# Decoder step: the last feed-forward's gate and up products of 18 slices as seven block products instead of eight

## The chip, the cores and the metric

The kernel runs on one core of a Trainium2 chip. The metric is the device time of one execution in microseconds (us). The engines have the names of the profile: PE (TensorE, matrix products), PEld (its weight loads), DVE (VectorE, elementwise), ACT (ScalarE, copies and functions), POOL (GpSimd), SP (the engine that issues nearly all transfers). PE reads its operands from the on-chip memory SBUF and writes to PSUM, eight banks of 2 KB per partition; DVE and ACT read both.

## The reference

A two-layer decoder step for one prompt of 1024 tokens and eight sample tokens, width 1024. Each layer is a mixer and then a feed-forward; the change touches only the second layer's feed-forward, for the second half of the prompt and the samples (512 + 8 = 520 columns).

```python
def swiglu(h, w_gu, w_down):
    gate, up = jnp.split(h @ w_gu, 2, axis=-1)
    return (jax.nn.silu(gate) * up) @ w_down
...
        h = h + rmsnorm(mix, g[1])
        h = h + rmsnorm(swiglu(rmsnorm(h, g[2]), w_gu[l], w_down[l]), g[3])
```

`w_gu` is 1024 x 5632 (2816 gate columns, then 2816 up columns), `w_down` 2816 x 1024. The 2816 columns are 22 slices of 128.

## The kernel before

**Layout and precision.** Activations are kept transposed: 128 features on the partitions, tokens along the row. Every fp32 operand of a product is split into a rounded high part (ACT) and the rest (DVE subtracts), and each 128x128 weight block takes three matmuls: high times high, high times low, low times high.

**Groups.** Group 0 is 512 prompt tokens, group 1 the other 512 and the 8 samples. A group-1 product is done as two column halves of 260, in the two banks of one PSUM tile.

**proj (L256 on)** makes one 128-row output: `split_w` (L240 on) loads the weights in tiles of four blocks (256 KB, SP queue, L245), splits them (L250 on ACT, L251 on DVE), and the matmuls of L264 follow. Five raw and five split weight tiles turn over (`wraw`, `wspl`).

**ffn.part (L464 on)** works through parts of 5, 5, 4, 4 and 4 slices. For a slice: gate product, SiLU (`silu`, L281 to L285: one DVE max, three ACT steps exp, ln, exp, one DVE product), up product, DVE product L474, split into the tile `m` (L271 on ACT, L272 on DVE). Then eight `w_down` products over the part's slices, added into the running sum `R` (L401 on ACT for the first part, L403 on DVE after it). `R` has one buffer for the whole kernel.

**PSUM.** Two tiles of two banks for products (`mmp`), three single banks (`smp`, `S()`) and one (`nsp`, `NS()`) for everything else.

**Order of work.** Pieces of the program are generators. `weave((a, na), (b, nb))` draws steps from both in the ratio na to nb, and `drain` runs one to its end. That is the program order, which a planner takes as priorities: with its own costs for every instruction it sets the order of each engine's queue, and the queues then run strictly in that order, with semaphores between them. Reuse of a buffer waits for the last reader of what was in it.

**The end of the program.** Around the change, in order: `f0.part(4)` of layer 1 for group 0, woven with `o1.finish` (which makes the input `x` of the last feed-forward); `f0.finish` (norm and residual, L384 and L390), `store_y` (transposes L1135 and the rows' store) and `token_rows` (transposes L440, L450), woven 22 to 18 with parts 0 and 1 of the last feed-forward `f1`; then `f1`'s parts 2, 3, 4, and `finish_rows`, which normalises and stores. Much earlier, layer 0's group-0 feed-forward is woven with the group-1 mixer.

POOL issues 32 indirect transfers for the sample cache (L731) and else nearly nothing.

Of the kernel before, what the change touches and what calls it, by code (L numbers as in the profile page):

```python
# [17 lines left out]
P = 128  # L18
# [4 lines left out]
def tile_decoder(  # L23
# [38 lines left out]
    mmp = pool("mmp", 2, space=PSUM)  # L62
    smp = pool("smp", 3, space=PSUM)
    nsp = pool("nsp", 1, space=PSUM)
# [15 lines left out]

    def NS():
        return nsp.tile([P, 512], F32, tag="ns", name=nm("ns"))
# [21 lines left out]
    def S():  # L104
        return smp.tile([P, 512], F32, tag="s", name=nm("s"))
# [209 lines left out]

    def wo_tiles(g):
        return [X(g) for _ in range(ND)]
# [136 lines left out]

    htok = []

    PARTS = [(0, 5), (5, 5), (10, 4), (14, 4), (18, 4)]

    class ffn:
# [4 lines left out]
        def part(self, pi):  # L464
# [18 lines left out]
            for m in range(ND):  # L483
                ps = proj(g, w_down[l], f0, nf, m * P, mids)
                evac_raw(g, self.R, ps, m, self.acc, pi == 0, last)
                if last and self.rows:
                    nc.scalar.activation(
                        self.R[m][:, :n], self.R[m][:, :n], AF.Copy, scale=gcol(l, 3, m)
                    )
                    if m == 3:  # L490
                        self.first_half()
# [11 lines left out]
        def first_half(self):  # L503
            self.yt = [xpool.tile([P, D], F32, tag="x0", name=nm("yT")) for _ in range(CH)]
            for c in range(CH):
                ps = S()
                for k in range(4):
                    nc.tensor.transpose(ps[:, k * P : (k + 1) * P], self.R[k][:, c * P : (c + 1) * P], ident)  # L508
                nc.scalar.copy(self.yt[c][:, :512], ps)
            self.ys = xpool.tile([P, D], F32, tag="x0", name=nm("yTs"))  # L510
            ps = S()
            for k in range(4):
                nc.tensor.transpose(ps[:NB, k * P : (k + 1) * P], self.R[k][:, G : G + NB], ident)
            nc.scalar.copy(self.ys[:NB, :512], ps[:NB, :])

        def finish_rows(self):

            ht, hsm = htok[0]
            g, R, acc = self.g, self.R, self.acc
            ps = NS()  # L520
            for c in range(CH):
                nc.tensor.matmul(ps[:, c : c + 1], acc[:, c * P : (c + 1) * P], ones[:, 0:1], start=True, stop=True)  # L522
            nc.tensor.matmul(ps[:NB, CH : CH + 1], acc[:, G : G + NB], ones[:, 0:1], start=True, stop=True)
            r = small([P, 8], tag="rr")
            nc.scalar.activation(r[:, :CH], ps[:, :CH], AF.Ln, scale=1.0 / D, bias=epsb)
            nc.scalar.activation(r[:, :CH], r[:, :CH], AF.Exp, scale=-0.5)
            rs = small([P, 8], tag="rr")
            nc.scalar.activation(rs[:NB, 0:1], ps[:NB, CH : CH + 1], AF.Ln, scale=1.0 / D, bias=epsb[:NB])
            nc.scalar.activation(rs[:NB, 0:1], rs[:NB, 0:1], AF.Exp, scale=-0.5)
            for c in range(CH + 1):  # L530
                prompt = c < CH
                n = P if prompt else NB
                yt, h = (self.yt[c], ht[c]) if prompt else (self.ys, hsm)
                rc = r[:, c : c + 1] if prompt else rs[:NB, 0:1]
                o = c * P
                pt = S()
                for k in range(4):
                    nc.tensor.transpose(pt[:n, k * P : (k + 1) * P], R[4 + k][:, o : o + n], ident)
                nc.vector.scalar_tensor_tensor(  # L539
                    yt[:n, :512], yt[:n, :512], rc, h[:n, :512], op0=ALU.mult, op1=ALU.add  # L540
                )
                nc.vector.scalar_tensor_tensor(  # L542
# [697 lines left out]
```

## Time and profile before

| | |
|---|---|
| median of 3 runs | 2549.02 us (2548.02 to 2551.21) |
| the profiled execution | 2551.36 us, span 2549.6 us, granted TensorE clock 0.996 |
| PE busy | 2518.9 us (99%), 15653 matmuls |
| DVE busy | 1557.2 us (61%) |
| ACT busy | 1186.6 us (47%) |
| POOL busy | 43.8 us (2%) |
| moved by DMA | 297.91 MB, mean 117 GB/s |

The span is the time from the first to the last instruction; the execution's own time is a little longer. Busy shares are means over stages of different kinds. In a group of instructions the first numbers are busy time and the mean of one in ns, and behind the bar stands the idle time of the engine just before them and what ended most of it. PE overlaps its matmuls, so the mean of one is longer than the step from one to the next; the step is the busy time of a stretch divided by its count. A row of the DMA queues has packets, MB and the share of 16 engines over the span that the packets took.

### The profile page before, as it was taken

To read this page: it belongs to the slowest core of one execution; us is meant where nothing else is said; L and a number is where in the kernel's file an instruction comes from. 1 tells how busy PE (TensorE), PEld (TensorE's weight loads), DVE (VectorE), ACT (ScalarE), POOL (GpSimd) and SP (SyncE) were. 2 spreads that over 40 slices of the span, in tenths; PEclk is the share of its full clock that TensorE was granted. 3 is DMA by queue.
4 is the path that set the end of the run, shared out by engine and by line. 5 is a ranking of instruction groups with operands and counts; after the bars stand their busy time and mean duration, and the time that the engine had idled before them with its cause. 6 is when DMAs were issued, how large, how long until landed. Compare 5 with 4: busy or idle time off the path is not lost. (4 is left out here: it accounts for less than half of the span.)

```text
span 2549.6 us, 40536 instructions
## 1 busy us (share of the span) xinstructions
PE 2518.9 (99%) x15653; PEld 2193.2 (86%) x15653; DVE 1557.2 (61%) x2714; ACT 1186.6 (47%) x2187; POOL 43.8 (2%) x59
## 2 busy tenths in 40 slices
PE   8999999999999999999999999999999999999998
PEld 6888898878877888999999989766776798999998
DVE  6666566654775677555544577667677558444445
ACT  6346543243443445555433455455555445443334
POOL 1000000000000000000000000011000000000000
PEclk9999999999999999999999999999999999999999
DMA  6352242233644445231333445453443244323332
GB/s 186 109 162 71 75 150 76 65 112 116 182 127 129 136 153 183 86 88 57 102 93 94 126 153 179 144 153 94 135 140 115 77 124 129 110 86 103 93 92 67
DMA packets 457708, 297.91 MB, mean 117 GB/s; under 512 B 17573, under 2 KB 422642, under 8 KB 457514
## 3 DMA queue, kind: packets, MB, share of 16 engines
q1 hardware_dynamic: 454954, 286.92, 37.6%
q0 software_dynamic: 2560, 8.39, 1.1%
q8 instruction: 123, 2.02, 0.3%
q14 instruction: 71, 0.58, 0.1%
HBM read 265.44 MB, written 29.80 MB: 116 GB/s over the span
## 5 line engine op out<-in xcount | busy, mean ns | idle before, releaser
L264 PE MATMUL mm<-x,ws 128*128 128x260 f32 (+1 forms) x10080 | 1668.4, 323 | 1.4 <-ACT x L355 1.3
L264 PEld LDWEIGHTS mm<-x,ws 128*128 128x128 f32 x10080 | 1443.1, 188 | 166.3 <-issue 29.2
L250 ACT CAST ws<-w 128x512 fp32r<-128x512 f32 (+1 forms) x800 | 475.5, 595 | 878.4 <-PE mm L264 801.3
L251 DVE TENSOR_TENSOR ws<-w,ws 128x512 fp32r<-128x512 f32 (+1 forms) x800 | 523.5, 657 | 324.0 <-ACT ws L250 314.6
L264 PE MATMUL mm<-m,ws 128*128 128x260 f32 (+1 forms) x3168 | 544.4, 326 | 0.1
L264 PEld LDWEIGHTS mm<-m,ws 128*128 128x128 f32 x3168 | 455.1, 189 | 53.9 <-issue 7.1
L403 DVE TENSOR_TENSOR r<-r,mm 128x520 f32<-128x520 f32 (+1 forms) x128 | 88.3, 690 | 99.2 <-PE mm L264 97.7
L281 DVE TENSOR_SCALAR t<-mm 128x512 f32<-128x512 f32 (+1 forms) x104 | 72.1, 693 | 102.5 <-PE mm L264 102.0
L474 DVE TENSOR_TENSOR t<-t,mm 128x512 f32<-128x512 f32 (+1 forms) x88 | 60.8, 691 | 117.2 <-PE mm L264 117.2
L285 DVE TENSOR_TENSOR t<-t,t 128x512 f32<-128x512 f32 (+1 forms) x88 | 61.1, 694 | 88.3 <-ACT t L284 88.1
L304 DVE TENSOR_TENSOR st<-st,n 128x512 f32<-128x512 f32 (+1 forms) x98 | 67.0, 690 | 6.9 <-ACT n L303 5.0
L272 DVE TENSOR_TENSOR m<-t,m 128x512 fp32r<-128x512 f32 (+1 forms) x88 | 61.0, 694 | 3.7 <-ACT m L271 1.6
L282 ACT ACTIVATE t<-t 128x512 f32<-128x512 f32 (+1 forms) x88 | 55.9, 635 | 14.9 <-DVE t L281 7.8
L271 ACT CAST m<-t 128x512 fp32r<-128x512 f32 (+1 forms) x88 | 54.8, 623 | 10.1 <-DVE t L474 2.8
L283 ACT ACTIVATE t<-t 128x512 f32<-128x512 f32 (+1 forms) x88 | 55.8, 635 | 2.6
L284 ACT ACTIVATE t<-t 128x512 f32<-128x512 f32 (+1 forms) x88 | 55.9, 635 | 2.4
L902 PEld LDWEIGHTS s<-a,a 128*128 128x128 f32 x448 | 53.4, 192 | 1.2
L902 PE MATMUL s<-a,a 128*128 128x64 f32 x448 | 53.2, 271 | 0.0
L1073 PE MATMUL s<-b,trir 128*128 128x512 f32 (+3 forms) x96 | 38.0, 397 | 7.6 <-DVE b L272 5.3
L731 POOL DMA_INDIRECT c<-in_cache_sb_k,pidx x16 | 16.2, 1015 | 1640.7 <-DVE x L272 790.4
L1037 DVE SCALAR_TENSOR_TENSOR b<-b,b 128x512 f32<-128x512 f32 (+3 forms) x48 | 26.7, 556 | 28.2 <-ACT b L1036 28.0
L1085 PE MATMUL s<-b,a 128*128 128x512 f32 (+3 forms) x96 | 41.6, 515 | 1.9 <-DVE b L1040 1.5
(298 smaller groups left out, 1940.2 us busy)
## 6 DMA issues: line engine op xcount, KB each, us to landing
w<-in_w_gu SPq DMA_DIRECT2D x352, 256.0 KB, 3.0
w<-in_w_down SPq DMA_DIRECT2D x160, 256.0 KB, 2.8
w<-in_w_in_a SPq DMA_DIRECT2D x80, 256.0 KB, 2.9
w<-in_w_o SPq DMA_DIRECT2D x64, 256.0 KB, 2.8
w<-in_w_mem_kv SPq DMA_DIRECT2D x32, 256.0 KB, 2.9
c<-in_cache_mem_k SPq DMA_DIRECT2D x16, 512.0 KB, 4.2
c<-in_cache_mem_v SPq DMA_DIRECT2D x16, 512.0 KB, 3.9
w<-in_w_kv SPq DMA_DIRECT2D x32, 256.0 KB, 3.1
```

The lines of the kernel that those rows point to most:

```text
L250: nc.scalar.copy(ws[:, 0, :n, :], raw[:, :n, :])
L251: nc.vector.tensor_sub(ws[:, 1, :n, :], raw[:, :n, :], ws[:, 0, :n, :].bitcast(F32))
L264: nc.tensor.matmul(ps[:, a, : PW[g]], wt, xt[k][:, xi, o : o + PW[g]], start=(k == 0 and wi == 0), stop=(k == nk - 1 and wi == 2),)
L272: nc.vector.tensor_sub(dst[1], src, dst[0].bitcast(F32))
L281: nc.vector.tensor_scalar(sv(x, g), pv(ps, g), -44.0, None, op0=ALU.max)
L282: nc.scalar.activation(d, x[:, :n], AF.Exp, scale=-1.0)
L284: nc.scalar.activation(d, d, AF.Exp, scale=-1.0)
L285: nc.vector.tensor_mul(d, d, x[:, :n])
L304: nc.vector.tensor_add(acc[:, :n], acc[:, :n], t[:, :n])
L403: nc.vector.tensor_add(dst, dst, pv(ps, g))
L474: nc.vector.tensor_mul(sv(sg, g), sv(sg, g), pv(pu, g))
L902: nc.tensor.matmul(plv[:, hh, c, :], K_[:, hh, cs], rhs, start=True, stop=True)
```

## The change

For 18 of the 22 slices, gate and up of a slice are no longer two products of 128 x 1024 by 1024 x 520. They are taken together as a two-by-two block product (gate and up rows; two halves of the 1024 inputs; two column halves of 260) and done with seven block products of 128 x 512 by 512 x 260 (Strassen's scheme in Winograd's form). A block product is 4 blocks x 3 matmuls = 12 matmuls, so a slice has 84 instead of 96.

- The four sums of weight blocks are made in DRAM: per part four tensors of 512 rows by the part's columns, by eight DMAs issued from POOL, four copies and four that add to what is there (`weight_sums`). They are woven into layer 0's group-0 feed-forward. Ahead of each part's eight, POOL copies one column of `f0.R[0]` (`mark`), behind which the eight are queued.
- The four sums of input blocks are made by DVE and split, for each of four row blocks (`sums_w`), behind slices 0, 1 and 2, whose products stay as they were in number (`gate_up_q`, slices 0 to 3).
- From slice 4 on, `gate_up_w` makes the slice: seven weight tiles of 256 KB (three from `w_gu`, four from the sums) instead of four, each split as before; partial results carried between PSUM banks by two negating ACT copies; two adds on DVE.
- All the PSUM pools are closed ahead of it and one of eight banks is opened (`quads`: four tags of two banks); `S()` and `NS()` take turns in two of the tags.
- SiLU is one ACT instruction for each half. From part 1 on, weight tiles also use buffers of the pools `a` and `c`.
- The weave of parts 0 and 1 with the work ahead goes from 22:18 to 17:7. `first_half` and `finish_rows` move out of the class unchanged; the down products use the banks of the new pool.

```diff
-    mmp = pool("mmp", 2, space=PSUM)
-    smp = pool("smp", 3, space=PSUM)
-    nsp = pool("nsp", 1, space=PSUM)
+    banks = ctx.enter_context(ExitStack())
+    mmp = banks.enter_context(tc.tile_pool(name="mmp", bufs=2, space=PSUM))
...
+    def Q(i):
+        return single[0].tile([P, 512], F32, tag=f"q{i}", name=nm("q"))
...
     def S():
+        if single:
+            turn[0] += 1
+            return Q(3 * (turn[0] % 2))
...
+    def sums_w(xs, ops):
+        n, h = NG[1], PW[1]
+        for k in range(4):
+            x0, x1 = xs[k], xs[k + 4]
...
+            def full(x, c):
+                t = B()
+                nc.vector.tensor_add(t[:, :h], x[:, 0, c : c + h].bitcast(F32), x[:, 1, c : c + h].bitcast(F32))
+                return t
+
+            b11, b12, b21, b22 = full(x0, 0), full(x0, h), full(x1, 0), full(x1, h)
+            for d, p, a, b in (
+                (b11, u[:, :, o : o + h], b12, b11), (b12, y[:, :, h : 2 * h], b12, b22),
+                (b22, y[:, :, :h], b22, b11), (b21, z[:, :, o : o + h], b21, b22),
+            ):
+                nc.vector.tensor_sub(d[:, :h], a[:, :h], b[:, :h])
+                split_to((p[:, 0, :], p[:, 1, :]), d[:, :h])
...
+    def gate_up_w(l, f, ops, spl, raws):
...
+        def product(ps, j, first=False):
+            w = split(weight(j))
+            i = src[j][1]
+            for k in range(4):
+                x = ops[k][i]
+                for wi, (wj, xi) in enumerate(((0, 0), (0, 1), (1, 0))):
+                    nc.tensor.matmul(
+                        ps[:, :h], w[:, wj, k * P : (k + 1) * P], x[:, xi, :],
+                        start=(first and k == 0 and wi == 0), stop=(k == 3 and wi == 2), skip_group_check=True,
+                    )
+
+        pa, pb, pc, pd = (Q(i) for i in range(4))
+        product(pa, 0, True)
+        nc.scalar.activation(pb[:, :h], pa[:, :h], AF.Copy, scale=-1.0)
+        product(pd, 1, True)
+        product(pb, 2)
+        nc.scalar.activation(pc[:, :h], pb[:, :h], AF.Copy, scale=-1.0)
+        product(pa, 3)
+        sg = T()
+        nc.scalar.activation(sg[:, :h], pa[:, :h], AF.Silu)
+        product(pb, 4)
+        dt = T()
+        nc.scalar.copy(dt[:, h:n], pd[:, :h])
+        gt = T()
+        nc.vector.tensor_add(gt[:, h:n], dt[:, h:n], pb[:, :h])
+        product(pc, 5)
+        nc.vector.tensor_sub(gt[:, :h], pc[:, :h], dt[:, h:n])
+        product(pb, 6)
+        nc.scalar.activation(sg[:, h:n], gt[:, :h], AF.Silu)
+        nc.vector.tensor_mul(sg[:, :h], sg[:, :h], pb[:, :h])
+        nc.vector.tensor_mul(sg[:, h:n], sg[:, h:n], gt[:, h:n])
...
+    def weight_sums(l, parts, after):
+        for i in parts:
+            mark = nc.gpsimd.tensor_copy(small([P, 1], tag="mk", bufs=1), after()[:, 0:1])
...
+            for d, a, add in (
+                (s3, a11, False), (s1, a21, False), (s3, a21, True), (s1, a22, True),
+                (s2, s3, False), (s2, a22, True), (s4, s2, False), (s4, a12, True),
+            ):
+                with tc.issue_after(mark.ins):
+                    if add:
+                        nc.gpsimd.dma_start(d, a, accum_op=ALU.add)
+                    else:
+                        nc.gpsimd.dma_start(d, a)
+                yield
...
+    class ffn_w:
...
+        def part(self, pi):
...
+                if f0 + j < self.plain:
+                    mt, ins = gate_up_q(l, f0 + j, self.x)
+                    mids.append(mt)
+                    with tc.issue_after(ins.ins):
+                        for _ in range((1, 2, 1, 0)[j]):
+                            next(self.sums, None)
+                else:
+                    mids.append(gate_up_w(l, f0 + j, self.ops, self.spl, self.raws))
...
-    weave((a1.sample(), 6), (a1.gate(), 4), (f0.part(1), 9))
-    weave((chain(a1.merge(), a1.mem()), 12), (a1.mem_sample(), 20), (chain(f0.part(2), f0.part(3)), 16))
-    drain(f0.part(4))
+    def running():
+        return f0.R[0]
+
+    weave((a1.sample(), 6), (a1.gate(), 4), (f0.part(1), 9), (weight_sums(1, (0,), running), 8))
+    weave(
+        (chain(a1.merge(), a1.mem()), 12), (a1.mem_sample(), 20), (chain(f0.part(2), f0.part(3)), 16),
+        (weight_sums(1, (1, 2), running), 16),
+    )
+    weave((f0.part(4), 8), (weight_sums(1, (3,4), running), 16))
...
-    f1 = ffn(1, 1, o1.x, True)
-    weave((chain(f0.finish(False), store_y(0, f0.R), token_rows(1, o1.R)), 22), (chain(f1.part(0), f1.part(1)), 18))
+    banks.close()
+    single.append(ctx.enter_context(tc.tile_pool(name="quads", bufs=2, space=PSUM)))
+    f1 = ffn_w(1, o1.x, 4)
+    weave((chain(f0.finish(False), store_y(0, f0.R), token_rows(1, o1.R)), 17), (chain(f1.part(0), f1.part(1)), 7))
     drain(f1.part(2), f1.part(3), f1.part(4), f1.finish_rows())
```

More of the change, by code (lines that the diff above doesn't have):

```diff
@@ L61, in tile_decoder @@
     cpool = pool("cpool", 4)
-    mmp = pool("mmp", 2, space=PSUM)
-    smp = pool("smp", 3, space=PSUM)
-    nsp = pool("nsp", 1, space=PSUM)
+    banks = ctx.enter_context(ExitStack())
+    mmp = banks.enter_context(tc.tile_pool(name="mmp", bufs=2, space=PSUM))
+    smp = banks.enter_context(tc.tile_pool(name="smp", bufs=3, space=PSUM))
+    nsp = banks.enter_context(tc.tile_pool(name="nsp", bufs=1, space=PSUM))
+    single = []
     uid = [0]
@@ L501, in finish, with first_half @@
                 yield
[L503 to L510, printed above, removed]
+    def first_half(self):
+        self.yt = [xpool.tile([P, D], F32, tag="x0", name=nm("yT")) for _ in range(CH)]
+        for c in range(CH):
@@ L511, in first_half @@
             ps = S()
             for k in range(4):
[L513 to L542, printed above, removed]
-                    yt[:n, 512:], pt[:n, :], rc, h[:n, 512:], op0=ALU.mult, op1=ALU.add
-                )
-                if prompt:
-                    t0 = g * G + c * P
-                    nc.sync.dma_start(y_prompt[0, t0 : t0 + P, :], yt)
-                else:
-                    nc.sync.dma_start(y_sample.rearrange("b o d -> (b o) d"), yt[:NB])
-                yield
```

167 lines of the change are left out of this document (166 added, 1 removed).

## The prediction

> **What bounds the kernel now.** I read the page's engines first, then its costliest groups, then the stretch in which the last feed-forward runs alone.
>
> ```profile
> PE 2518.9 (99%) x15653; PEld 2193.2 (86%) x15653; DVE 1557.2 (61%) x2714; ACT 1186.6 (47%) x2187; POOL 43.8 (2%) x59
> ...
> L250 ACT CAST ws<-w 128x512 fp32r<-128x512 f32 (+1 forms) x800 | 475.5, 595 | 878.4 <-PE mm L264 801.3
> ```
>
> PE is never without work; ACT's weight splits wait for PE to give split tiles back (801.3 us), so loads and splits run ahead. The stretch from slice 5 to near the end, and its groups by shape:
>
> ```profile
> 2297.62:2521.78 224.16, 224.16 (x1875) 224.16 (x1874) 107.65 (x162) 85.56 (x140) 0.00 (x0) 1.00 0.31 90
> ```
> ```profile
> L264 PE MATMUL mm<-x,ws 128*128 128x260 f32 x1152 | 138.2, 282 | 0.0
> ...
> L251 DVE TENSOR_TENSOR ws<-w,ws 128x512 fp32r<-128x512 f32 x78 | 54.0, 692 | 23.8 <-ACT ws L250 22.8
> L250 ACT CAST ws<-w 128x512 fp32r<-128x512 f32 x78 | 48.5, 621 | 123.8 <-PE mm L264 123.6
> ...
> L272 DVE TENSOR_TENSOR m<-t,m 128x520 fp32r<-128x520 f32 x13 | 9.1, 700 | 0.9 <-ACT m L271 0.3
> L474 DVE TENSOR_TENSOR t<-t,mm 128x520 f32<-128x520 f32 x13 | 9.0, 696 | 20.3 <-PE mm L264 20.3
> L285 DVE TENSOR_TENSOR t<-t,t 128x520 f32<-128x520 f32 x12 | 8.4, 701 | 16.8 <-ACT t L284 16.8
> L281 DVE TENSOR_SCALAR t<-mm 128x520 f32<-128x520 f32 x12 | 8.4, 699 | 18.3 <-PE mm L264 18.3
> L271 ACT CAST m<-t 128x520 fp32r<-128x520 f32 x13 | 8.2, 628 | 1.3
> ```
>
> The columns of the first row are PE, PEld, DVE and ACT busy with their counts, POOL, the granted clock, the DMA share and GB/s. PE is busy for all 224.16 us at full clock: 1875 matmuls, 119.6 ns from one to the next, no idle before them. DVE is at 48%, ACT at 38%. Here a matmul less is 119.6 ns less, as long as nothing else becomes late.
>
> **The saving.** 18 slices lose 96 - 84 = 12 matmuls of 128x260 each: 216 x 0.1196 = 25.8 us. The Trainium skill, "TensorE: Matmul & The Clock Gate", section "Wait — 56ns, not 53.3ns?", gives a warm matmul N / 2.4 GHz plus about 2.5 ns: for 260 columns that is 110.8 ns by estimate, and the saving would be 23.9 us. The trace's step is 8.8 ns longer than that, and the measured step is taken.
>
> **ACT and DVE in a Strassen slice.** Halves of 260 have no row; short shapes give the slope:
>
> ```profile
> L250 ACT CAST ws<-w 128x128 fp32r<-128x128 f32 x64 | 19.0, 297 | 91.9 <-PE mm L264 84.7 <-issue 5.3 <-ACT b L643 1.5
> L251 DVE TENSOR_TENSOR ws<-w,ws 128x128 fp32r<-128x128 f32 x64 | 18.5, 289 | 49.7 <-ACT ws L250 49.5
> ```
>
> Between 128 and 512 elements ACT goes from 297 to 621 ns, DVE from 289 to 692: at 260 about 0.41 and 0.43 us. ACT per slice: seven splits 4.35, two negating copies, one copy and two SiLU 2.05, the split of `m` 0.63: 7.0 us. DVE: seven 4.84, four at 0.43 1.72, 0.70: 7.3 us. PE: 84 x 0.1196 = 10.05 us. PE stays the longest, and SiLU's three ACT steps and two DVE steps that go had been off the path: nothing is gained by them. Whether ACT reloads a function table for SiLU no row says; a load or two has about a slice's spare 3 us on ACT: nothing.
>
> **Weight supply.** Seven tiles (1.84 MB) in 10.05 us are 183 GB/s, twice the 90 of the row above. A stretch with that flow exists:
>
> ```profile
> DMA packets 15988, 11.60 MB, mean 184 GB/s; under 512 B 616, under 2 KB 13928, under 8 KB 15984
> ...
> q1 hardware_dynamic: 15984, 11.55, 61.8%
> ...
> w<-in_w_gu SPq DMA_DIRECT2D x18, 256.0 KB, 2.9
> ```
>
> From 637 to 700 us the weights land 2.9 us after issue at 61.8% of the engines. A raw tile is held for about 2.9 + 0.62 + 0.69 = 4.2 us; one is wanted each 1.44 us, so three would do; slice 4 has five, later slices thirteen. The far row is the group with 7.2 us:
>
> ```profile
> w<-in_w_in_b SPq DMA_DIRECT2D x32, 256.0 KB, 7.2
> ```
>
> With that, five tiles give one in 1.7 us, and slice 4 loses 7 x 0.26 = 1.9 us. Between 0 and 1.9; I take 0, the nearer row being of the same weights. SP waits for DVE's splits, as before.
>
> **Chains inside a slice.** Between the products stand two negating copies and a DVE add, each covered by one other product, 12 x 0.1196 = 1.44 us: the copy `pb` (product 2 needs it), the copy `pc` (product 4 overwrites its source), the add `gt` (product 6 overwrites it). A result is there 0.16 us after the step (282 against 119.6 ns), the copy takes 0.41, the handovers some 0.1: 0.67 us. With one split (0.62) in progress on that queue 1.29, still covered; with two ahead 1.91, and PE waits 0.46. 18 x 3 = 54 chains: from 0 to 24.8 us. The planner puts the copy ahead of later splits; I take one in four late by 0.2: 2.7 us.
>
> **New PSUM pool.** I take it that no bank of `quads` is used before the last tile of the closed pools has been read.
>
> ```profile
> 2144.54 3.94 PE L264 MATMUL mm<-x,ws 128*128 128x260 f32 x31
> ...
> 2145.53 0.68 DVE L403 TENSOR_TENSOR r<-r,mm 128x512 f32<-128x512 f32 x1
> ```
>
> Now slice 0 begins at 2144.54, while the last down product is still to be added, done at 2146.2. PE waits there: 1.7 us; 0 if the banks come free singly. Inside the new pool `S()` shares banks with products; its tiles were the bound nowhere here: 0.
>
> **The input sums.** `sums_w` issues 48 DVE instructions of 0.43: 20.6 us, and 16 ACT splits of 0.41, before slice 4's second product. DVE in the first four slices:
>
> ```profile
> 2144.00:2156.00 12.00, 12.00 (x93) 11.19 (x92) 11.96 (x20) 7.94 (x14) 0.00 (x0) 1.00 0.17 50
> 2156.00:2168.00 12.00, 12.00 (x103) 12.00 (x102) 12.00 (x21) 5.27 (x9) 0.00 (x0) 1.00 0.46 132
> 2168.00:2180.00 12.00, 12.00 (x103) 12.00 (x102) 6.63 (x11) 5.04 (x8) 0.00 (x0) 1.00 0.32 93
> 2180.00:2192.00 12.00, 12.00 (x103) 12.00 (x101) 5.88 (x9) 5.43 (x9) 0.00 (x0) 1.00 0.23 67
> ```
>
> DVE is already full for 24 us with the residual of group 0. It has 36.5 us of work in 48. A plain slice drops from 4 x 0.69 + 2.80 to 4 x 0.69 + 0.86 + 0.70, four of them 5.0 us; with 20.6 that makes 52.1 us in 48: slice 4 is late by 4, more with its first splits. PE can fill that with transposes that came after it:
>
> ```profile
> 2210.07 3.91 PE L1135 MATMUL s<-ident,r 128*128 128x128 f32 x32
> ...
> 2259.53 1.03 PE L440 MATMUL s<-ident,a 128*128 128x128 f32 x8
> ```
>
> They are 3.9 and some five times 0.9 us, and 17:7 lets them come earlier. From 0 (filled) to 6; I take 3.
>
> **The weight sums.** 40 transfers in layer 0, hidden unless they hold PE's weights or DVE. Their engines' price, from the page's queue rows, and POOL's:
>
> ```profile
> q1 hardware_dynamic: 454954, 286.92, 37.6%
> q0 software_dynamic: 2560, 8.39, 1.1%
> ...
> L731 POOL DMA_INDIRECT c<-in_cache_sb_k,pidx x16 | 16.2, 1015 | 1640.7 <-DVE x L272 790.4 <-PE s L632 437.2 <-DVE sc L691 405.0
> ```
> ```profile
> 475.00:530.00 55.00, 54.98 (x352) 46.66 (x351) 30.56 (x79) 20.45 (x38) 0.00 (x0) 1.00 0.28 79
> ...
> 615.00:692.00 77.00, 77.00 (x365) 63.92 (x364) 55.53 (x87) 34.92 (x62) 0.00 (x0) 1.00 0.55 165
> ```
>
> q0: 1.1% of 2549.6 us for 8.39 MB, 3.3 us per MB. A five-slice tensor is 1.31 MB: 4.4 us, 8.0 with the engines 45% busy; adding, which also reads its destination, 8 to 16. Landing adds 2.0 (2.9 less 0.9 of moving), POOL's issue 1.0 (a row of 128 descriptors) to 4.1 (four times as many). A copy step is 11 to 14 us, an adding one 11 to 22. The eighth issue of a part stands behind five such steps (three copies, two adds), with two more transfers beside: 11 to 21 us a step; I take 16. All of it ends by about 930 us, and the sums are first read after 2190: no wait there. PE in that stage: weights landing later are covered by ten tiles (5 raw, 5 split). 0 to 6, as sample loads on which DVE waits also land later; I take 2.
>
> **Tail.** Two adds of 0.43 for one of 0.70 behind the last matmul: 0.2 us more.
>
> ```profile
> 2535.99 0.71 DVE r L403
> ```
>
> **Sum.** -25.8 + 2.7 + 1.7 + 3 + 2 + 0.2 = -16.2. The profiled execution took 2551.36, 2.3 over the median 2549.02: 2535.2 on its own terms, 2533 for the median.
>
> **Rivals.** (1) The chains eat the gain. If each of the 54 waits 0.3 us, 16.2 go instead of 2.7, and the time is about 2546; at 0.46, 2555. For it: both queues are 70% full with splits of 0.62 and 0.69, in strict order. Against: one split fits.
>
> (2) Slower, by the marks. POOL's copy of `R[0]` stands in its queue behind the issues of the part before, and the next writer of `R[0]` on DVE waits for that copy. The writers now:
>
> ```profile
> 617.87 0.68 DVE L403 TENSOR_TENSOR r<-r,mm 128x512 f32<-128x512 f32 x1
> ...
> 856.04 0.69 DVE L403 TENSOR_TENSOR r<-r,mm 128x512 f32<-128x512 f32 x1 [0.83 <-PE mm L264]
> ...
> 884.13 1.41 DVE L384 SCALAR_TENSOR_TENSOR r<-r,par,st 128x512 f32<-128x512 f32 x2 [1.09 <-ACT st L295]
> ```
> ```profile
> 809.39 43.71 PE L264 MATMUL mm<-x,ws 128*128 128x512 f32 x192
> ```
>
> Part 1's mark runs at 618.6 at the earliest; part 4's comes 5 + 4 + 4 steps of length D later (parts of four slices are 0.8 as long), 618.6 + 13 D, and must be ahead of L384 at 884.1: D = 20.4 us is the point. Five split tiles of 12 x 0.228 us cover 13.7 us more, and the gain is used up at D = 22.7. At 24 us DVE is 46 late, PE 33: 2566. My ends for D are 11 and 21.
>
> (3) Slower, weights starved. A sum is 32 rows of 2.56 KB on each engine, 137 ns each by q0's rate; a weight tile is 32 runs of 34 ns (q1: 37.6% of 16 x 2549.6 us for 454954). If the engines take turns, a sum lasts 5.5 us and lets one tile pass, where PE uses two. The 2 us pause behind each waited sum lets two more pass; without pauses, beyond the ten tiles, 40 sums cost up to 30 x 2.7 = 82 us: 2615. The chain of waits speaks against it. The Trainium skill, "DMA: Bandwidth & Descriptors", section "Queues, rings and completion order", says that an engine goes round between its queues packet by packet; no row here shows the two queues both loaded.
>
> **Chances.** Forecast 0.66 (2522 to 2542). Rival 1 0.16, of it 0.10 within 0.2% (5 us, about what a measurement here can tell from no change) and 0.06 slower. Rival 2 0.10, rival 3 0.04, a stage of input sums far longer than counted 0.04, halved between same and slower. Low end: no cost at all, 2523.2, less 2.2 for the spread of the runs; high end 2560, past rival 1, which leaves out some 0.15.
>
> **What would show it.** In the new profile: 15437 matmuls; about 84 per 10 us from part 1 on, with PE idle before the matmuls of products 2, 4 and 6 (ACT and DVE releasers) at 2.7 us in all; one gap of 1.7 us ahead of slice 0; a gap at slice 4 released by DVE; R's writers at 856 and 884 where they were. Wrong it would be by PE idle in layer 0 put down to POOL or to late weights, or by a matmul step other than 119.6 ns.

## The result and the profile after

The changed kernel is slower: 2567.60 us median of five executions (2565.68 to 2579.99), against 2550.27 us of five executions of the kernel before (2548.02 to 2551.21). The ratio is 1.0083, 95% interval 1.0058 to 1.0109. The forecast was 2533 us with a range of 2521 to 2560, so the time lies outside it, on the other side of the kernel before. The profiled execution took 2567.60 us, span 2565.9 us, 16.3 more than before.

Engines and DMA queues on the page of the changed kernel:

```profile
PE 2513.8 (98%) x15437; PEld 2175.1 (85%) x15437; DVE 1593.6 (62%) x2860; ACT 1215.0 (47%) x2302; POOL 79.2 (3%) x104
...
q1 hardware_dynamic: 483466, 301.08, 39.6%
q0 software_dynamic: 16224, 54.53, 8.6%
```

15437 matmuls, as the change says, and PE's busy time fell by 5.1 us only, where 216 matmuls less should give 25.8. PE went from 99% to 98% of a longer span. Both say that the loss is on PE, in part as longer steps and in part as idle time.

The matmuls of both kernels stand in the same order up to number 12361, the first of the last feed-forward. So the start of the k-th matmul in one trace less that in the other is the delay up to that point. In us, by the time in the kernel before:

```
time in the kernel before   470    537    618    704    798    883   1023   1250   1555   2000   2100   2144.5
changed kernel              3.2    3.2    4.2   18.5   34.5   35.3   36.3   36.5   37.0   37.9   38.2   40.4
```

At slice 0 of the last feed-forward the changed kernel is 40.4 us late (2184.98 against 2144.54). Of these, some 30 come between 618 and 798 us, in layer 0, where the weight sums are made. From slice 0 to the last down product it then gains: 2144.54 to 2535.99 were 391.45 us, 2184.98 to 2550.90 are 365.92, which is 25.5 us less. The tail behind that gives 1.4 back (2550.90 to 2565.9 is 15.0 us, 2535.99 to 2549.6 was 13.6). 40.4 - 25.5 + 1.4 = 16.3.

The stretch 640 to 800 us by windows, first the kernel before and then the changed one (PE, PEld, DVE, ACT, POOL busy with counts, granted clock, DMA share, GB/s):

```profile
640.00:800.00 160.00, 160.00 (x694) 122.83 (x693) 110.64 (x170) 64.82 (x124) 0.00 (x0) 1.00 0.51 151
```
```profile
640.00:800.00 160.00, 140.58 (x567) 107.92 (x566) 91.75 (x142) 54.64 (x104) 10.03 (x13) 0.93 0.87 226
```

PE was busy all the time and did 694 matmuls; now it does 567. By that count 160 x (1 - 567/694) = 29.3 us of work are missing. PE idles for 19.4 us. The granted clock, 0.93 as the mean of the window, is 0.50 in four stretches of it, 23.9 us together, in which PE is busy for 17.7: half of that, 8.9 us, is lost. The two make 28.3; the last 1.0 is about what the slower steps take in this window (they are told under "The drift"). The Trainium skill, "TensorE: Matmul & The Clock Gate", section "Part 1: The HAM clock gate", has the clock fall after an idle stretch and come back after a few us of work. The trace agrees in kind: the four stretches begin in or right behind gaps of 3.4 to 7.0 us, the gap of 1.6 us has none, and in the same window before, without gaps, the clock is 1.00. So here the gaps cost nearly half as much again as they are long.

What the engines wait for, by the table of waits of the changed kernel from 600 to 800 us (engine, line waited for, us, times, longest):

```profile
DVE ws L263 <- ACT ws L262: 24.7, 10, 6.4
...
DVE c L918 <- DMA b<-qd: 18.0, 3, 11.6
...
DVE c L930 <- DMA c<-in_cache_mem_v: 13.1, 4, 6.8
...
PE mm L276 <- DVE r L448: 12.2, 3, 7.0
ACT ws L262 <- DMA w<-in_w_gu: 8.4, 8, 6.2
```

DVE stands behind loads of the sample mixer's queries and cache, ACT behind raw weights that haven't come, and PE behind DVE, which has yet to empty its PSUM banks (L448 is the add into `R`; L257, L262, L263 and L276 are what were L245, L250, L251 and L264). None of these rows names a sum: only POOL's own queue waits for the sums, and the others wait for the transfers beside them. PE has five gaps from 640 to 800 us. The first two (1.6 and 3.6 us) go back over DVE and ACT to weight tiles that hadn't come, the next two (3.4 and 7.0) over DVE to loads of `qd`, the last (3.8) over DVE to a load of the cache. One late weight tile, and the longest gap behind its load:

```profile
655.68 0.62 ACT L262 CAST ws<-w 128x512 fp32r<-128x512 f32 x1 [6.18 <-DMA w<-in_w_gu]
...
739.32 1.23 DVE L918 TENSOR_TENSOR c<-c,b 128x1024 f32<-128x1024 f32 x1 [11.64 <-DMA b<-qd]
...
741.20 5.41 PE L276 MATMUL mm<-m,ws 128*128 128x512 f32 x12 [7.01 <-DVE r L448]
```

The transfers from 640 to 700 us, in 40 slices of 1.5 us, before and after:

```profile
DMA  6465274657897889995589966888952505050514
...
q1 hardware_dynamic: 15335, 11.23, 62.9%
```
```profile
DMA  9999999968999999999996689999999999999999
...
q1 hardware_dynamic: 12557, 9.44, 56.3%
q0 software_dynamic: 1921, 7.13, 51.2%
```

Before, the engines are 63% busy, in bursts up to 9 tenths with room between. After, the packets of q1 and q0 add up to 107% (the times of packets overlap somewhat), and there is no room. Over 475 to 1000 us a weight tile of `w_gu` now lands 8.1 us after its issue (2.9 in the same stretch before), and a sum, by the page, after 10.5 to 11.7:

```profile
w<-in_w_gu SPq DMA_DIRECT2D x68, 256.0 KB, 8.1
```
```profile
wsum<-in_w_gu POOLq DMA_DIRECT2D x18, 1024.0 KB, 10.5
...
wsum<-in_w_gu POOLq DMA_DIRECT2D x12, 1280.0 KB, 11.7
```

The price of a sum comes from the queue rows: q0 takes 8.6% of 2565.9 us less the 1.1% of 2549.6 it took before, 192.6 us of 16 engines for 46.14 MB: 4.2 us per MB. By packets it is 16 x 192.6 us over 13664, 226 ns. If an engine takes turns, each of the 32 runs of a weight tile (34 ns) stands behind one such packet: 32 x (0.034 + 0.226) = 8.3 us, and 8.1 is measured. The packets show the turns directly: first from 661 to 665 us, with a sum under way, then from 654 to 657 us, in the pause ahead of that sum.

```profile
q0 software_dynamic: 273, 0.70, 91.7%
q1 hardware_dynamic: 254, 0.13, 16.7%
```
```profile
q1 hardware_dynamic: 1757, 0.87, 112.9%
q0 software_dynamic: 6, 0.00, 0.1%
```

Under the sum the two queues send packets one for one, 273 to 254, and q1 sends 64 in a us; in the pause it sends 586. A weight tile is 512 packets of 512 bytes: 8.1 us at the first rate, 0.9 at the second. The Trainium skill, "DMA: Bandwidth & Descriptors", section "Queues, rings and completion order", has an engine go round between its queues packet by packet; these counts agree with it.

### The profile page after: what moved, and what is told of

It reads as the page before. It is cut to its first block, busy times and chain, and to the rows that moved or that the text cites. A ratio compares the mean times of both kernels' runs of the same rounds, so it can differ in the third digit from the quotient of the medians.

```text
span 2565.9 us, 40498 instructions
## 1 busy us (share of the span) xinstructions
PE 2513.8 (98%) x15437; PEld 2175.1 (85%) x15437; DVE 1593.6 (62%) x2860; ACT 1215.0 (47%) x2302; POOL 79.2 (3%) x104
## 5 line engine op out<-in xcount | busy, mean ns | idle before, releaser
L276 PE MATMUL mm<-x,ws 128*128 128x260 f32 (+1 forms) x7968 | 1430.7, 335 | 7.4 <-DVE r L448 3.6
L276 PEld LDWEIGHTS mm<-x,ws 128*128 128x128 f32 x7968 | 1194.1, 189 | 183.6 <-issue 32.3
L262 ACT CAST ws<-w 128x512 fp32r<-128x512 f32 x728 | 429.9, 592 | 726.3 <-PE mm L276 583.2
L263 DVE TENSOR_TENSOR ws<-w,ws 128x512 fp32r<-128x512 f32 x728 | 474.7, 655 | 312.5 <-ACT ws L262 303.1
L276 PE MATMUL mm<-m,ws 128*128 128x512 f32 (+1 forms) x2112 | 419.0, 349 | 8.6 <-DVE r L448 8.6
L276 PEld LDWEIGHTS mm<-m,ws 128*128 128x128 f32 x2112 | 329.6, 190 | 63.2 <-DVE r L448 9.2
L666 PE MATMUL q<-m,ws 128*128 128x260 f32 x1056 | 128.8, 283 | 0.0
L666 PEld LDWEIGHTS q<-m,ws 128*128 128x128 f32 x1056 | 127.2, 188 | 0.4 <-ACT hT L486 0.2
L544 DVE TENSOR_TENSOR ws<-w,ws 128x512 fp32r<-128x512 f32 x126 | 86.5, 692 | 60.2 <-ACT ws L543 54.9
L553 PE MATMUL q<-y,ws 128*128 128x260 f32 x864 | 112.9, 283 | 0.0
L543 ACT CAST ws<-w 128x512 fp32r<-128x512 f32 x126 | 77.9, 621 | 68.1 <-PE q L666 27.0
L553 PEld LDWEIGHTS q<-y,ws 128*128 128x128 f32 x864 | 107.6, 188 | 0.0
L448 DVE TENSOR_TENSOR r<-r,mm 128x512 f32<-128x512 f32 (+1 forms) x96 | 66.1, 689 | 64.9 <-PE mm L276 63.9
L283 ACT CAST m<-t 128x512 fp32r<-128x512 f32 (+1 forms) x88 | 54.8, 623 | 22.5 <-DVE t L702 13.6
## 6 DMA issues: line engine op xcount, KB each, us to landing
wsum<-in_w_gu POOLq DMA_DIRECT2D x18, 1024.0 KB, 10.5
wsum<-in_w_gu POOLq DMA_DIRECT2D x12, 1280.0 KB, 11.7
```

Source lines behind the costliest of these rows:

```text
L262: nc.scalar.copy(ws[:, 0, :n, :], raw[:, :n, :])
L263: nc.vector.tensor_sub(ws[:, 1, :n, :], raw[:, :n, :], ws[:, 0, :n, :].bitcast(F32))
L276: nc.tensor.matmul(ps[:, a, : PW[g]], wt, xt[k][:, xi, o : o + PW[g]], start=(k == 0 and wi == 0), stop=(k == nk - 1 and wi == 2),)
L283: nc.scalar.copy(dst[0], src)
L448: nc.vector.tensor_add(dst, dst, pv(ps, g))
L543: nc.scalar.copy(w[:, 0, :], src)
```

## The experiments

Two theories stood at the start. **Sums**: the bytes of the 40 transfers hold up other loads in layer 0. **New feed-forward**: the Strassen stage itself, or what it does to the planner's order, costs the time. Later others came up, from the marks to the sizes of SBUF slots. Delays below are against the kernel before, at matmuls counted as above.

### Without the sums

The 40 transfers, their marks and their waits are gone; the last feed-forward reads its seven tiles from `w_gu`.

```diff
-            (w_gu[l][0:512, gate : gate + P], 0), (sums[l][part][0][:, o : o + P], 4), (sums[l][part][1][:, o : o + P], 5),
-            (w_gu[l][512:D, gate : gate + P], 1), (sums[l][part][2][:, o : o + P], 6), (sums[l][part][3][:, o : o + P], 2),
+            (w_gu[l][0:512, gate : gate + P], 0), (w_gu[l][0:512, up : up + P], 4), (w_gu[l][512:D, up : up + P], 5),
+            (w_gu[l][512:D, gate : gate + P], 1), (w_gu[l][0:512, up : up + P], 6), (w_gu[l][0:512, gate : gate + P], 2),
...
-    weave((a1.sample(), 6), (a1.gate(), 4), (f0.part(1), 9), (weight_sums(1, (0,), running), 8))
+    weave((a1.sample(), 6), (a1.gate(), 4), (f0.part(1), 9))
```

> Leaves out the sums of the weights in DRAM; the seven products take tiles straight from w_gu, so the last feed-forward is computed with wrong weights, with the same count and size of loads. Theory A (the bytes of the sums hold up weights and sample loads in layer 0, the last feed-forward itself keeps its saving): about 38 us under the changed kernel, 2529 us, and PE in layer 0 as it was before. Rival C (the last feed-forward does not bring its 25.8 us): 2540 us or more.

Measured: 2534.26 us (2533.53 to 2535.76), ratio 0.9937 (0.9921 to 0.9954). The delay is 2.1 us at 618, 3.4 at 798, 5.3 at 1023 and 6.3 at slice 0. So the jump of 30 us is gone with the sums, and a slow drift is left, which the sums don't make; it is about the 5 us by which the time exceeds theory A's 2529.

### The sums alone

The kernel before, with the 40 transfers and the marks woven in as in the change, and nothing reading the sums.

```diff
+    weave((a1.sample(), 6), (a1.gate(), 4), (f0.part(1), 9), (weight_sums(1, (0,), running), 8))
...
+    weave((f0.part(4), 8), (weight_sums(1, (3,4), running), 16))
```

> The kernel before with the 40 transfers and the marks, their results unused. Theory A: 38 us over the kernel before, 2588 us. Rival C (most of the loss lies in the last feed-forward): under 2565 us.

Measured: 2585.87 us (2583.55 to 2587.89), ratio 1.0140 (1.0123 to 1.0157). The delay is 0.2 at 470, 8.0 at 537, 21.5 at 704, 34.8 at 798, and stays there: 34.8 at 1250, 32.2 at slice 0. The sums cost 32 to 35 us in the kernel before too, and there is no drift here. Some 8 of these come ahead of 537 us, where the changed kernel loses nothing to them.

### All transfers, few bytes; then half the bytes

The marks, the 40 issues and all their waits stay, but each transfer has 16 of its 512 rows, and in a second run 256. As in the first run, the last feed-forward reads its tiles from `w_gu`.

```diff
-                        nc.gpsimd.dma_start(d, a, accum_op=ALU.add)
+                        nc.gpsimd.dma_start(d[0:16], a[0:16], accum_op=ALU.add)
...
-                        nc.gpsimd.dma_start(d, a)
+                        nc.gpsimd.dma_start(d[0:16], a[0:16])
```

> As e1, but with all 40 transfers, marks and waits issued, each cut from 512 rows to 16 (the products take tiles from w_gu, so the last feed-forward is computed with wrong weights). Theory A (it is the bytes): as e1, about 2530 us. Rival B (POOL's marks, the waits between the transfers or the other order of the queues cost the time): as the changed kernel, about 2567 us.

> The changed kernel with the same 40 transfers, marks and waits in the same place, but each carries only the first 256 of the 512 rows of its sum; the last feed-forward reads its seven weight tiles from w_gu itself, so its products aren't those of the reference and the time alone is read. With 16 rows the time was 2537.8, with 512 rows (the changed kernel) 2567.6. Theory T (threshold: up to what the DMA engines have free in this stretch the transfers cost nothing): half the bytes bring the DMA share of 640 to 800 us from 1.0 to about 0.8, and the time is 2536 to 2543. Theory L (each byte delays the others, in proportion): half of the loss of 30 us stays, 2551 to 2555. With T the shift against the kernel before stays under 10 us at the 798th us, with L it is about 20.

Measured with 16 rows: 2537.77 us (2535.99 to 2538.96), ratio 0.9951 (0.9934 to 0.9967). It is hardly the marks, the issues or the waits; it is what the transfers carry. (At 883 us this run is 2.8 us later than the one without transfers, 1.1 of it already at 150 us, ahead of the first transfer; so marks, issues and waits cost some 2 us at most.) Measured with 256 rows: 2542.02 us (2537.91 to 2542.49), ratio 0.9964 (0.9950 to 0.9978), and 12.0 us late at 883 where 16 rows are 7.1 late and the full sums 35.3. Half of the bytes cost 5 us, all of them 28. That is no fixed price per byte: the loss grows much faster than the bytes. Whether there is a threshold these runs don't tell. The window with half of the bytes:

```profile
640.00:800.00 160.00, 156.49 (x667) 118.36 (x666) 107.54 (x165) 63.89 (x122) 11.28 (x16) 1.00 0.69 192
```

At a DMA share of 0.69 PE idles 3.5 us; at 0.87 (all bytes, above) 19.4. And where PE's gaps are short, the granted clock stays at 1.00.

### One transfer per step of the stage

The same place, but a mark of its own ahead of each transfer, so that the 40 spread over the whole stage instead of running in lots of eight.

```diff
         for i in parts:
-            mark = nc.gpsimd.tensor_copy(small([P, 1], tag="mk", bufs=1), after()[:, 0:1])
...
             ):
+                mark = nc.gpsimd.tensor_copy(small([P, 1], tag="mk", bufs=1), after())
                 with tc.issue_after(mark.ins):
...
     def running():
-        return f0.R[0]
+        return f0.tick
```

`tick` is a column of what was made last, a slice's `m` or a tile of `R`.

> All of the change, the sums where the change has them, but with a mark ahead of each transfer (behind the last slice or down product of layer 0's group-0 feed-forward) instead of one per part. If what hurts is transfers back to back that keep the engines full: 2540 to 2548 us. If it is the place, with DVE waiting in its queue for sample loads: 2560 us or more.

Measured: 2567.16 us (2565.68 to 2570.64), ratio 1.0062 (1.0045 to 1.0079). The delay falls from 18.5 to 4.4 at 704 and from 35.3 to 21.1 at 883, but it is 40.6 at 1023. By the total the loss has only moved:

```profile
640.00:800.00 160.00, 152.23 (x639) 116.27 (x638) 102.04 (x157) 60.11 (x116) 17.22 (x26) 0.97 0.87 235
800.00:960.00 160.00, 141.15 (x751) 118.25 (x750) 87.28 (x140) 63.81 (x115) 29.57 (x44) 0.96 0.95 250
```

But the second half of it has another cause, which this run brings in itself. Of PE's 18.9 idle us in the second row, 14.9 lie between 920 and 947 us. There DVE's residual step (L429, which was L384) is to overwrite a tile of `R` that a mark has yet to read, and the mark stands in POOL's queue behind a transfer that waits for the one before it:

```profile
920.06 1.42 DVE L429 SCALAR_TENSOR_TENSOR r<-r,par,st 128x512 f32<-128x512 f32 x2 [5.93 <-POOL mk L602]
...
938.19 0.75 DVE L429 SCALAR_TENSOR_TENSOR r<-r,par,st 128x512 f32<-128x512 f32 x1 [12.49 <-POOL mk L602]
...
939.60 4.36 PE L276 MATMUL mm<-x,ws 128*128 128x260 f32 x22 [10.24 <-DVE ws L263]
```

That is the mechanism of the prediction's rival 2. The delay grows by 19.5 us from 883 to 1023, where other runs drift by 1.0; without the other 18.5 the time would by estimate be 2549 us, just over the first theory's range. Up to 883 us, with 30 of the 40 transfers issued (32 in the changed kernel), spreading halved the loss: 14 us over the run with 16 rows instead of 28. So this run doesn't decide between its two theories; spreading helped, and its marks took the gain back.

### The sums in the next stage

All of the change, with the sums in layer 0's group-1 feed-forward instead, one transfer to a step.

```diff
+    weave(
+        (chain(b0.sb(), b0.mem()), 24), (chain(f1.part(0), f1.part(1)), 18),
+        (weight_sums(1, (0, 1), running), 16),
+    )
+    weave((chain(f1.part(2), f1.part(3), f1.part(4)), 24), (weight_sums(1, (2, 3, 4), running), 24))
```

> All of the change, but the sums are made in layer 0's group-1 feed-forward (no sample loads, DMA share 0.21 to 0.35), one transfer behind each of its steps, with a mark ahead of each. Theory A, with single transfers some 9.6 us apart covered by the weight tiles loaded ahead: 2530 us, up to 2540 if single transfers still hold up weights. Rival B: 2565 us or more, as there are more marks.

Measured: 2537.81 us (2535.71 to 2538.12), ratio 0.9947 (0.9930 to 0.9963). The same 46 MB now cost next to nothing: the delay is 8.0 at 1023 and 8.4 at 1435, that is 0.4 us over the stage with the sums. The stage from 1060 to 1440 us without the sums (the run without them), and with them:

```profile
1060.00:1440.00 380.00, 379.31 (x2951) 363.99 (x2950) 200.13 (x356) 174.32 (x329) 3.79 (x4) 1.00 0.31 89
```
```profile
1060.00:1440.00 380.00, 379.19 (x2945) 363.48 (x2945) 199.87 (x357) 173.89 (x329) 46.66 (x70) 1.00 0.74 188
```

The engines of DMA go from 0.31 to 0.74 and PE loses nothing, with weight tiles landing after 5.2 us. In the first stage the base was 0.51. The share alone doesn't decide: with half of the bytes it was 0.69 there, and 5 us were lost. The stages differ in more than the base. The second has no loads of `qd` or of the memory cache for DVE to wait for, and here the transfers come one to a step and not in lots of eight. Which of these saves the 28 us no run separates. Moved and spread, the sums turn the change from a loss into a gain.

### The tail: the function tables

In the changed kernel, and in the run just told, two table loads stand on ACT behind the last product, on the chain that ends last (start, duration, engine and line; changed kernel):

```profile
2553.11 1.28 ACT L753 ACT_TABLE_LOAD   x1
2554.82 1.28 ACT L754 ACT_TABLE_LOAD   x1
```

They come back to the tables of ln and exp after SiLU. The code asks for that load ahead of the last down products, but the planner doesn't leave the request there, and no load stood at its line. The run holds it in its place.

```diff
-                nc.scalar.preload_act_table_set("natural_log_exp_and_others")
+                tc.keep_in_program_order(nc.scalar.preload_act_table_set("natural_log_exp_and_others"))
```

> As e4, and the load of ACT's table for ln and exp stays in program order behind the last slice's SiLU instead of floating ahead of it. The two table loads of 1.28 us that stand behind the last product leave the tail: 2.6 us under e4, 2535 us. If a load of the tail is hidden behind DVE anyway: as e4, 2538 us.

Measured: 2538.14 us (2537.31 to 2539.68), ratio 0.9951 (0.9935 to 0.9968). The two loads are gone from the tail, which is 13.5 us where it was 15.0; but the time isn't less than that of the run before it (2537.81). The delay had been larger already at 150 us (2.6 against 1.4), so something early in this execution, whose cause is open, takes the 1.5 us back. The tail is shown, a gain in time is not.

### The drift: slots of 4160 bytes

The runs with the new feed-forward told so far drift in layer 0, those without sums in that stage too: they are 5.3, 8.0 and 9.2 us late at 1023. Their input sums (`y`, 2 x 520 elements) share the slots of group 0's x tiles (2 x 512), which grow from 4096 to 4160 bytes per partition, for the whole kernel. The run gives the kernel before such slots and changes nothing else.

```diff
-            self.yt = [xpool.tile([P, D], F32, tag="x0", name=nm("yT")) for _ in range(CH)]
+            self.yt = [xpool.tile([P, 2 * WID], F32, tag="x0", name=nm("yT"))[:, :D] for _ in range(CH)]
```

> The kernel before with one size changed: the buffers of group 0's products get 4160 bytes per partition instead of 4096, as the new operand tiles of the change make them. Theory W (that size makes the 512-column matmuls on these buffers 3.7 ns longer, 3360 of them): 233 ns instead of 229.6 from one to the next, 2555 to 2562 us. Rival: as before, 2550 us, and the slow matmuls come from something else in the changed kernel.

Measured: 2558.27 us (2557.94 to 2560.92), ratio 1.0033 (1.0020 to 1.0046): slower by 8 us with the same instructions. One stretch of 192 matmuls of 512 columns on such tiles, the kernel before and this one:

```profile
809.39 43.71 PE L264 MATMUL mm<-x,ws 128*128 128x512 f32 x192
```
```profile
815.81 44.54 PE L264 MATMUL mm<-x,ws 128*128 128x512 f32 x192
```

227.7 ns become 232.0 ns each, with no idle between. Over all 3360 such matmuls the step, long gaps left out, goes from 229.6 to 233.2 ns; in the changed kernel it is 233.3. 3360 x 3.6 ns would be 12 us; 8 are seen, and where the rest goes is open.

### Wider slots again, and what it takes to have room

The kernel with the sums in the next stage and the table load held, and slots of 4352 bytes. The room is made in two ways: with four raw weight tiles instead of five, and then with five and six `b` buffers (working tiles of ACT and DVE) instead of seven. In the second, the slots of `m` are also widened, from 4160 to 4224 bytes.

```diff
-        return xpool.tile([P, 2, NG[1]], F32R, tag="x0", name=nm("y"))
+        return xpool.tile([P, 2, 544], F32R, tag="x0", name=nm("y"))[:, :, : NG[1]]
...
-    wraw = pool("wraw", 5)
+    wraw = pool("wraw", 4)
```
```diff
-    bpool = pool("bpool", 7)
+    bpool = pool("bpool", 6)
...
-        return mpool.tile([P, 2, WID], dt, tag="m", name=nm("m"))
+        return mpool.tile([P, 2, WID + 8], dt, tag="m", name=nm("m"))[:, :, :WID]
```

> As e5, with the same buffers padded to 4352 bytes, a multiple of 256, and four raw weight tiles instead of five to make room. Theory W with the remainder by 256 as its reason: the step goes back to 229.6 ns, 2527 to 2531 us. If the reason is another one, or four raw tiles are too few: 2535 us or more.

> The change with the weight sums in layer 0's second feed-forward (group 1) and the table load kept early, as two runs before, and three sizes besides: the slots of group 0's x tiles 4352 bytes, those of m tiles 4224 (a multiple of 128 instead of 4160), all five raw weight tiles kept, and six b buffers instead of seven to make the room. Theory (slots decide the step of 512-column matmuls): the x0 matmuls keep 229.6 ns, those on m fall from 235.6 to 229.6 too; layer 0 and layer 1 have some 2 x 176 x 3 x ... m matmuls of 512 columns, 4 to 5 us less; with five raw tiles the losses of 6.2 us (1022 to 1132 us) and 2.6 us (1435 to 1555 us) of the run with four go, at least by half. 2525 to 2530 us. Rival (the number of raw tiles had nothing to do with these losses, they come from the engines of DMA under the sums): the loss of some 6 us under the sums stays, and 2529 to 2533 us. Rival (seven b buffers were needed): DVE waits for b buffers in the mixers of both layers, 2535 us or more.

Measured with four raw tiles: 2534.34 us (2533.41 to 2537.69), ratio 0.9940 (0.9923 to 0.9956). The step is 229.5 ns again and the delay 0.5 us up to 883; but 6.2 us go between 1023 and 1132, where the sums begin, and 2.6 between 1435 and 1555. The 6.2 go in one place, behind a late weight tile:

```profile
1116.78 0.62 ACT L262 CAST ws<-w 128x512 fp32r<-128x512 f32 x1 [4.86 <-DMA w<-in_w_down]
...
1118.78 0.67 PE L1288 MATMUL s<-a,a 128*128 128x128 f32 x2 [4.83 <-DVE x L284]
```

Measured with five and six `b` buffers: **2526.11 us (2524.33 to 2528.66), ratio 0.9905 (0.9889 to 0.9922)**, the fastest of all. The delay is 0.5 us at 1132 and 1.5 at slice 0:

```profile
2146.05 2.03 PE L511 MATMUL q<-x,ws 128*128 128x260 f32 x15 [1.75 <-DVE r L448]
```

Of the 6.2 us nothing is left, of the 2.6 some 1.1. So the seventh `b` buffer isn't needed, and with the transfers of the sums under way the fifth raw tile most likely is; the slots of `m` differ between the two runs as well. The step of the 512-column matmuls on `m` did not change (235.3 ns; 235.6 before), so that part of the expectation missed.

### Which slot size

Last, `m` slots of 4352 bytes and x0 slots of 4224, the reverse of the run before.

```diff
-        return mpool.tile([P, 2, WID + 8], dt, tag="m", name=nm("m"))[:, :, :WID]
+        return mpool.tile([P, 2, WID + 24], dt, tag="m", name=nm("m"))[:, :, :WID]
...
-        return xpool.tile([P, 2, 544], F32R, tag="x0", name=nm("y"))[:, :, : NG[1]]
+        return xpool.tile([P, 2, 528], F32R, tag="x0", name=nm("y"))[:, :, : NG[1]]
```

> As the run before with five raw tiles and six b buffers, but the slots of m tiles are 4352 bytes (there 4224) with the low half starting 2176 bytes into the slot (there 2112), and the slots of group 0's x tiles are 4224 bytes (there 4352; their low half starts at 2048). Theory A (an operand row that starts at a multiple of 128 bytes takes the short step): the 1056 matmuls of 512 columns on m fall from 235.3 to about 229.6 ns, those on x0 keep 229.6, the time falls by some 6 us to 2519 to 2522. Theory B (multiples of 256 are needed): m falls to 229.6 (4352 and 2176 give 256 for the high half alone: 232), x0 rises to 233, 3360 x 3.7 ns = 12 us more and 2 to 6 less: 2532 to 2537. Theory C (m's longer step has another cause, such as its place in the program): m stays at 235.3, and with x0 as before the time is that of the run before, 2524 to 2528.

Measured: 2537.86 us (2537.12 to 2541.65), ratio 0.9951 (0.9935 to 0.9968). A stretch of 87 matmuls on x0 in the run before (4352) and in this one (4224):

```profile
198.26 20.30 PE L276 MATMUL mm<-x,ws 128*128 128x512 f32 x87
```
```profile
200.66 20.77 PE L276 MATMUL mm<-x,ws 128*128 128x512 f32 x87
```

With the pauses between groups in them these are 233.3 and 238.7 ns each; the step without long gaps is 233.8 in this run. No theory holds whole: x0 did as theory B said, `m` as theory C. So on x0 4096 and 4352 bytes (16 and 17 times 256) have the short step, 4160 and 4224 the long one; a multiple of 128 is not enough. On `m` it stays at 235.5: its longer step has a cause that no run here found. Whether it is the slot's size or the address that follows from it the runs don't separate.

## Why the prediction was wrong, point by point

**The step that failed** is "The weight sums": "0 to 6, as sample loads on which DVE waits also land later; I take 2". Measured are 32 to 35 us with the sums alone and 28 more than with 16 rows in the changed kernel, five times the upper end. Three things were wrong in it.
- The price was sized at 3.3 us per MB, from q0's indirect loads; it is 4.2. That alone is no great matter.
- The share of the engines was taken as a mean: 0.55 over the part, with room for the sums. On the mean they do fit: 0.51 of the stretch 640 to 800 was in use, and the sums' queue took 41.8% of it. But the stage's own loads come in bursts, which the 40 slices of 640 to 700 us show, and a tile issued in a burst lets a packet of the sum pass ahead of each of its own.
- "weights landing later are covered by ten tiles" didn't hold, and it counted the weights alone. Of the 19.3 us of PE's five gaps, 5.1 go back to late weight tiles, 10.4 to DVE's loads of `qd` and 3.8 to one of the cache. Each time PE waits for DVE, whose queue runs in order and stood behind such a wait.

**Rival 3** (weights starved) had the mechanism and was given 0.04. Its turn-taking gave 32 x (34 + 137) ns = 5.5 us for a sum and for a tile; with the measured packet it is 8.3 for a tile, and 8.1 is seen. The pauses that argued it down ("The 2 us pause behind each waited sum lets two more pass") are there (1757 packets of q1 in 3 us, above), but they don't suffice: of its 82 us without pauses about 30 came true, in the stretches in which the stage's own loads were dense. "The chain of waits speaks against it" was a chain of a trace in which q0 had almost nothing to do; it could not speak to this.

**Rival 2** (the marks) falls for the changed kernel. POOL waits for `R`, and nobody waits for POOL's marks (marks in the changed kernel, POOL's timeline):

```profile
622.85 0.58 POOL L592 COPY mk<-r 128x1 f32<-128x1 f32 x1 [95.22 <-DVE r L448]
...
892.18 0.57 POOL L592 COPY mk<-r 128x1 f32<-128x1 f32 x1 [20.45 <-DVE r L448]
```

Part 1's eighth transfer is issued at 674.09, its first at 623.38: 50.7 us for five steps, 10 us each, a little under the 11 to 21 given and far from the 20.4 at which it would decide. With a mark ahead of each transfer the rival did come true, for some 18 us.

**Rival 1** (the chains) falls too. Four parts of Strassen slices on the chain that ended last:

```profile
2278.94 50.43 PE q L553 x420
...
2358.07 40.34 PE q L553 x336
...
2421.41 40.37 PE q L553 x336
...
2484.82 40.35 PE q L553 x336
```

171.49 us for 1428 matmuls are 120.1 ns each: 0.5 over the step counted with, 0.7 us for all 18 slices, where 2.7 were taken. No product waits for its copy: PE is busy without a gap from 2190 to 2537 us. In the run with five raw tiles and slots of 4352 bytes such a part takes 40.21 us, 119.7 ns a matmul, so even these 0.7 go with the slots and not with the chains.

```profile
2382.67 40.21 PE q L553 x336
```

**The saving** was right: 25.5 us measured from slice 0 to the end of the products, 25.8 counted. The weight supply, ACT's and DVE's load and the SiLU steps cost nothing, as written.

**The new PSUM pool**: 1.7 us predicted, 1.76 measured:

```profile
2184.98 2.04 PE L511 MATMUL q<-x,ws 128*128 128x260 f32 x15 [1.76 <-DVE r L448]
```

**The input sums**: 0 to 6 us, 3 taken; measured is 0, the lower end. DVE is full for 36 us, but PE never waits for it:

```profile
2196.00:2208.00 12.00, 12.00 (x103) 12.00 (x102) 12.00 (x27) 5.07 (x11) 0.00 (x0) 1.00 0.38 109
2208.00:2220.00 12.00, 12.00 (x102) 12.00 (x101) 11.96 (x32) 6.67 (x15) 0.00 (x0) 1.00 0.18 50
```

**The tail**: 0.2 us predicted, 1.4 measured, by the two table loads; the text had looked for loads among the slices only. Without them the tail is 13.9 us (2511.86 to 2525.8 in the fastest run), 0.3 over before.

**Not seen at all** was the slots' size: the prediction named "a matmul step other than 119.6 ns" as a sign of error, but looked for it in the new stage. It came in the old ones, on tiles that the change doesn't touch, 8 us in the kernel before.

With the sums moved, the slots mended and the table held, the change is worth 23.4 us against the kernel before measured beside it (2549.53), of the 25.5 that the products save. The rest is the 1.75 of the banks, the tail's 0.3 and small shifts. That is 7 us beyond the forecast: it had counted 2.7 for the chains, 3 for the input sums and 2 for the weight sums, and none of the three is there.

## What to carry to other kernels

Before background transfers are put into a stage, look at its DMA share in slices of about a tile's flight time, not as a mean, and count which loads have a reader waiting: here 46 MB cost 28 to 35 us over a base of 0.51 with bursts, and 0.4 over a base of 0.31 with the transfers spread. A chain of waits tells nothing about a queue that is idle in that trace. A mark that reads a tile holds up the tile's next writer for as long as it stands in its own queue. And when a new tile shares a pool's slots, compare the slot's size before and after: every reader of the pool is affected.

## What was not expected of the hardware

- The step of a 512-column fp32 matmul on group 0's x tiles goes with the slot size of these tiles: 229.6 ns for 4096 and 4352 bytes, 233.2 to 233.8 for 4160 and 4224, with the same instructions. The 260-column matmuls on `y` tiles, in the same slots, show less of it: 120.6 ns at 4160, 120.2 at 4224, 119.7 and 119.8 at 4352. On `m` the step stays at 235.3 to 235.6 at 4160, 4224 and 4352.
- The loss from background transfers is not in proportion to bytes: 5 us for half of them, 28 for all.
- The five executions of the changed kernel span 14 us, those of the kernel before 3. The other two starved kernels (sums alone, one transfer per step) span 4 and 5, so the cause of the 14 is open.
- Gaps in PE's work can cost more than their length, through the clock: from 640 to 800 us 19.4 us of gaps and 8.9 us of lower clock; with half of the bytes 3.5 us of gaps, of 1.5 at most, left the clock at 1.00.
